# Second down pair of a decoder block: six of eleven blocks by seven products instead of five, and plain steps moved ahead of the splits of sums

## The chip, the cores and the metric

The kernel runs on one core of a Trainium2 chip. A core has five engines that work side by side and wait for each other by semaphores: TensorE (PE, matmuls), VectorE (DVE), ScalarE (ACT), GpSimd (POOL, here only an issuer of DMAs) and SyncE (SP, the issuer of most DMAs). The metric is the device time of one execution in microseconds (us), as a median of runs.

## The reference

One decoder layer on 256 tokens of width 2048, in float32. The part that the change touches is the last line: the gated activations, 256 x 5632, times `w_down`, 5632 x 2048, added to `x`.

```python
D_MODEL = 2048
SEQ = 256
D_FF = -(-(8 * D_MODEL) // (3 * 256)) * 256      # 5632
...
    x = x + merged @ w_out

    h2 = rmsnorm(x, g_ffn)
    gu = h2 @ w_gu
    x = x + (jax.nn.silu(gu[..., :D_FF]) * gu[..., D_FF:]) @ w_down
    return x
```

## The kernel before

PE multiplies in a fast format, and float32 accuracy is had by splitting each operand into a high and a low part: `split` (L109) casts the high part on ACT and subtracts it on DVE to get the low part. Each weight tile of 256 rows x 512 columns (`w_raw` or `g_raw`, 512 KB) is loaded by a DMA that SP issues, split once (`parts`, L322), and used by `product` (L177 to L179), three matmuls of 512 columns for each 128 x 128 piece of activations. The five pairs of `w_hi` and `w_lo` buffers are how far the splits can run ahead of PE.

The down projection is done in two pairs of 512 columns each (`down_pair`, L1163 on): the first call makes columns 0 to 1023, the second 1024 to 2047. The 5632 rows are eleven blocks of 512. A block's part in a pair is a 2 x 2 product of quarters (two halves of 128 tokens, two halves of 256 rows, two halves of 512 columns), and there are two ways to do it:

- plain, four steps (`rest`): a weight quarter is split and meets both halves of tokens, 12 matmuls a step, 48 in all;
- by sevens (`seven`): a scheme of seven products instead of eight. Each `form` splits one quarter or one sum of quarters and multiplies it by one piece of activations or of their sums, 6 matmuls a form, 42 in all. Its weights are b11 (form 1), u = b11 + b12 (form 5), u + b22 (form 6), b22 (form 3), b21 (form 2), b12 + b22 (form 7) and u + b22 + b21 (form 4). In the second pair the first two sums are made by DVE (L1203, L1207), the sum b12 + b22 (L1223) and the last sum of u (L1229) by DMAs that add into their target, issued by POOL; in the last block by sevens that last sum is DVE's (L1227).

Blocks 4, 6 and 8 have their sums of activations from the first pair. The second pair also takes blocks 3 and 5 by sevens: when a plain block (0, 1) is done, `sums_again` reads the raw activations of block 3 or 5 back (`a_raw`), re-makes the sums by four small differences on DVE (L231 to L236) and splits them into the done block's buffers.

`by_sevens` is a generator over the blocks by sevens. In the second pair every `yield True` (or `yield bool(again)`) in `seven` lets one plain step be written there, so that the long plain steps stand among the short forms. A scheduler at build time then sets the order on each engine from this order of writing; `tc.keep_in_program_order` holds an instruction at its place.

Of the kernel before, what the change touches and what calls it, by code (L numbers as in the profile page):

```python
# [30 lines left out]
NB = 512  # L31
# [25 lines left out]
def hybrid_block(ctx: ExitStack, tc: tile.TileContext, x, w_in, w_branch, w_out, w_gu, w_down, rel_bias,  # L57
                 onehot, extra, across, factors, out):
    nc = tc.nc
# [32 lines left out]
    def half_kb(dt=F32):  # L92

        return scratch.tile([P, NB], dt, name="sc")
# [77 lines left out]
    def product(ps, ah, al, wh, wl, start=False, stop=False, half=None):  # L172
        how = dict(skip_group_check=True)
        wh, wl = woven(wh), woven(wl)
        if half is not None:
            ps, wh, wl = ps[:, HALVES[half]], *(a[:, half * NB // 4:(half + 1) * NB // 4] for a in (wh, wl))
        nc.tensor.matmul(ps, ah, wh, start=start, stop=False, **how)  # L177
        nc.tensor.matmul(ps, ah, wl, start=False, stop=False, **how)  # L178
        nc.tensor.matmul(ps, al, wh, start=False, stop=stop, **how)  # L179
# [136 lines left out]
    def load(w, k, col0, pl=None):  # L316

        raw = pl.tile([P, 2, NB], F32, name="g_raw", bufs=6 if pl is gx else 4) if pl else wpool.tile([P, 2, NB], F32, name="w_raw", bufs=4)
        (nc.sync.dma_start if w is w_down else fetch)(raw, block(w, k, col0))
        return raw  # L320

    def parts(src):  # L322
        hi = wpool.tile([P, 2, NB], F32R, name="w_hi")
        lo = wpool.tile([P, 2, NB], F32R, name="w_lo")
        with tc.issue_after(fence.pop().ins) if fence else nullcontext():
            split_last[:] = split(hi, lo, src)
        advance(stages)
        split_count[0] += 1
        if split_count[0] % 2:
            advance(slow_stages)  # L330
        return hi, lo
# [5 lines left out]
    def snapshot(ps):  # L337
        sb = half_kb()
        nc.scalar.copy(sb, ps)  # L339
        return sb  # L340
# [709 lines left out]
    WD = (4, 6, 8)  # L1050
# [101 lines left out]
    def sums_again(c, room):  # L1152
        raw = pr.tile([P, 4, S], F32, name="a_raw", bufs=2)
        nc.gpsimd.dma_start(raw, a_mem[c])
        for _ in range(4):
            yield
        sums(*(raw[:, :, t * P:(t + 1) * P] for t in range(NT)), True)
        yield
        split(*a.t[room], raw, True)
        a.s[c] = a.t[room]  # L1160
        yield

    def down_pair(c0, mine, spare, queues, sevenths, again={}):  # L1163


        own = dict(zip(((0, 0), (1, 0), (0, 1), (1, 1)), mine()))
        begun, apart = set(), []
        xc = {}
        for t in range(NT):
            for n in range(2):  # L1170
                xc[t, n] = half_kb()
                nc.gpsimd.dma_start(xc[t, n], x1[t, :, c0 + n * NB:c0 + (n + 1) * NB])

        def into(ps, lhs, wh, wl, last=False, half=None):
            for j in range(2):
                product(ps, *lhs(j), wh[:, j], wl[:, j], id(ps) not in begun, last and j == 1, half)
                begun.add(id(ps))

        def rest(c, n, kh, last=False):
            k = 4 * c + 2 * kh  # L1180
            wh, wl = parts(load(w_down, k, c0 + n * NB))
            for t in range(NT):
                if last and again and n and t:
                    begun.discard(id(apart[0]))
                    for half, ps in enumerate((own[t, n], apart[0])):
                        into(ps, lambda j: a.plain(t, k + j), wh, wl, last, half)
                else:
                    into(own[t, n], lambda j: a.plain(t, k + j), wh, wl, last)

        def form(ps, f, c, src, last=False):  # L1190
            wh, wl = parts(src)
            into(ps, lambda j: a.form(f, c, j), wh, wl, last)

        def seven(c, f1, f5, f6, f7, last):
            def quarter(kh, n):
                return load(w_down, 4 * c + 2 * kh, c0 + n * NB, gd)

            b11 = quarter(0, 0)
            form(f1, 1, c, b11, last)
            yield bool(again)  # L1200
            b12 = quarter(0, 1)
            u = gd.tile([P, 2, NB], F32, name="u", bufs=1)
            tc.keep_in_program_order(nc.vector.tensor_add(u, b11, b12))  # L1203
            form(f5, 5, c, u, last)
            yield bool(again)
            b22 = quarter(1, 1)
            nc.vector.tensor_add(u, u, b22)  # L1207
            if not again:
                form(f6, 6, c, u, last)
                yield  # L1210
                nc.vector.tensor_add(b12, b12, b22)
                form(f7, 7, c, b12, last)
                yield
                form(own[0, 1], 3, c, b22)
                yield
                b21 = quarter(1, 0)
                form(own[0, 0], 2, c, b21)
                yield
                nc.vector.tensor_add(u, u, b21)
                form(own[1, 0], 4, c, u)  # L1220
                yield
                return
            nc.gpsimd.dma_start(b12, b22, accum_op=ALU.add)  # L1223
            form(f6, 6, c, u, last)
            b21 = quarter(1, 0)
            if last:
                tc.keep_in_program_order(nc.vector.tensor_add(u, u, b21))  # L1227
            else:
                nc.gpsimd.dma_start(u, b21, accum_op=ALU.add)  # L1229
            yield True  # L1230
            form(own[0, 1], 3, c, b22)
            yield
            form(own[0, 0], 2, c, b21)
            yield
            form(f7, 7, c, b12, last)
            yield True
            form(own[1, 0], 4, c, u)
            yield

        def combine(f1, f5, f6, f7):  # L1240

            s1 = snapshot(f1)
            nc.vector.tensor_add(xc[0, 0], xc[0, 0], s1)
            nc.vector.tensor_add(s1, f6, s1)
            s3 = half_kb()
            nc.vector.tensor_add(s3, f7, s1)
            s5 = snapshot(f5)
            yield
            nc.vector.tensor_add(xc[1, 0], xc[1, 0], s3)
            nc.vector.tensor_sub(s1, s5, s1)  # L1250
            nc.vector.tensor_add(xc[0, 1], xc[0, 1], s1)
            nc.vector.tensor_sub(s3, s5, s3)
            nc.vector.tensor_add(xc[1, 1], xc[1, 1], s3)
            yield

        def by_sevens():
            f = spare()
            apart.extend(f[:1] if again else ())
            for c in sevenths:
                yield from seven(c, *f, c == sevenths[-1])  # L1260
            yield from combine(*f)

        sevens = by_sevens()
        plain = [(c, n, kh) for c in ORDER if c not in sevenths for kh in range(2) for n in range(2)]
        if not again:
            for i, at in enumerate(plain[:-4]):
                rest(*at)
                if i >= 6:
                    next(sevens, None)
        steps = iter(plain[:-4] if again else [])  # L1270
        for now in sevens:
            at = next(steps, None) if now else None
            if at:
                rest(*at)
                if at[0] in again and at[1:] == (1, 1):
                    stages.append(sums_again(again[at[0]], at[0]))
        for at in steps:
            rest(*at)
        for n in range(2):
            for kh in range(2):  # L1280
                rest(plain[-1][0], n, kh, kh == 1)
            for t in range(NT):
                y = xc[t, n]
                if apart and t and n:
                    nc.vector.tensor_add(y, own[t, n], y)
                for half, cols in enumerate(HALVES):
                    if not (apart and t and n):
                        nc.vector.tensor_add(y[:, cols], own[t, n][:, cols], y[:, cols])
                    elif half:
                        nc.vector.tensor_add(y[:, cols], apart[0][:, cols], y[:, cols])  # L1290
                    queues[half].dma_start(
                        out[t * P:(t + 1) * P, c0 + n * NB + cols.start:c0 + n * NB + cols.stop], y[:, cols])
# [5 lines left out]
        return [acc2.tile([P, NB], F32, name=n) for n in "zv"] + [tr.tile([P, NB], F32, name="tr") for _ in range(2)]  # L1298

    down_pair(0, in_acc, elsewhere, (nc.scalar, nc.gpsimd), WD)  # L1300
    down_pair(2 * NB, elsewhere, in_acc, (nc.sync, nc.scalar), WD + (3, 5), {0: 3, 1: 5})


_INS = ["x", "w_in", "w_branch", "w_out", "w_gu", "w_down", "rel_bias"]
# [33 lines left out]
```

## Time and profile before

| | |
|---|---|
| runs | 1335.63, 1335.96, 1336.26 us, median 1335.96 |
| profiled execution | 1335.64 us, of it 1333.9 us span from first to last instruction |
| PE busy | 1327.6 us, 100% of the span |
| DVE busy | 1176.0 us, 88% |
| ACT busy | 946.2 us, 71% |
| DMA reading and writing HBM | 232 GB/s over the span |
| second down pair on PE | from 1222.67 us to the end |

An engine's busy time says how much of the span it had an instruction at work. PE is full in every slice, so where PE never waits the time follows from its number of matmuls. Whether another engine is close to making it wait has to be read from the order of time in a stage.

### The profile page before, as it was taken

What the parts mean: (1) busy time and instruction counts of PE and PEld (TensorE: products, weight loads), DVE (VectorE), ACT (ScalarE), POOL (GpSimd) and SP (SyncE); (2) the same over time, 40 slices, a digit from 0 to 9 for tenths busy, and PEclk for the clock granted to TensorE, in tenths of its full rate; (3) what the DMA queues carried; (4) which work ended last, traced back from release to release, by engine and by line L of the source; (5) the groups of instructions that cost most, each with busy time, mean ns of one, the idle gap of its engine ahead of it and who ended that gap; (6) DMA issues with size and microseconds to landing.
All of it is one profiled execution on the core that took longest, in us unless ns stands there. A gap on an engine that the chain in (4) does not pass through costs nothing.

```text
span 1333.9 us, 17798 instructions
## 1 busy us (share of the span) xinstructions
PE 1327.6 (100%) x6243; PEld 1158.4 (87%) x6243; DVE 1176.0 (88%) x1261; ACT 946.2 (71%) x1216; POOL 132.4 (10%) x197
## 2 busy tenths in 40 slices
PE   9999999999999999999999999999999999999998
PEld 6888888888888888888888888888888888888887
DVE  7978898989888897888999999998889997998887
ACT  6786867788777776546778778777877876665563
POOL 1100110001111111110210000001000001001010
PEclk9999999999999999999999999999999999999999
DMA  9987977897789878887988889889899977789893
GB/s 359 307 284 243 263 211 256 254 282 215 263 267 289 275 245 276 297 304 255 284 314 268 273 257 275 234 260 302 280 286 278 270 222 256 250 276 303 269 273 96
DMA packets 119793, 355.75 MB, mean 267 GB/s; under 512 B 32864, under 2 KB 34584, under 8 KB 119704
## 3 DMA queue, kind: packets, MB, share of 16 engines
q1 hardware_dynamic: 77016, 277.45, 57.9%
q0 software_dynamic: 20272, 70.81, 22.7%
q10 hardware_dynamic: 22416, 6.36, 3.0%
q8 instruction: 49, 0.80, 0.2%
q14 instruction: 40, 0.33, 0.1%
HBM read 294.26 MB, written 14.70 MB: 232 GB/s over the span
## 4 chain that ended last, share of the span: by engine, by line
PE 97%; DVE 1%; DMA 1%; ACT 0%; issue 0%; SPq 0%; DVEq 0%; ACTq 0%
PE qs L178 12%; PE qs L177 12%; PE qs L179 12%; PE ps L178 11%; PE ps L179 11%; PE ps L177 11%; PE z L177 4%; PE z L179 4%; PE z L178 4%; PE v L177 3%; PE v L179 3%; PE v L178 3%; PE tr L179 1%; PE tr L177 1%; PE tr L178 1%; PE tr L210 1%
## 5 line engine op out<-in xcount | busy, mean ns | idle before, releaser
L109 DVE TENSOR_TENSOR w_lo<-w_raw,w_hi 128x1024 fp32r<-128x1024 f32 x298 | 361.5, 1222 | 45.6 <-ACT w_hi L109 44.4
L109 ACT CAST w_hi<-w_raw 128x1024 fp32r<-128x1024 f32 x298 | 309.3, 1047 | 95.8 <-PE qs L179 26.0
L109 ACT CAST w_hi<-g_raw 128x1024 fp32r<-128x1024 f32 x220 | 227.0, 1050 | 105.7 <-PE qs L179 32.9
L109 DVE TENSOR_TENSOR w_lo<-g_raw,w_hi 128x1024 fp32r<-128x1024 f32 x220 | 262.7, 1223 | 19.4 <-ACT w_hi L109 16.9
L109 ACT CAST w_hi<-u 128x1024 fp32r<-128x1024 f32 x165 | 172.1, 1049 | 116.9 <-DVE u L1203 21.3
L109 DVE TENSOR_TENSOR w_lo<-u,w_hi 128x1024 fp32r<-128x1024 f32 x165 | 199.8, 1224 | 45.0 <-ACT w_hi L109 40.1
L178 PE MATMUL qs<-w_lo,h_hi 128*128 128x512 f32 x348 | 132.6, 381 | 0.0
L179 PE MATMUL qs<-w_hi,h_lo 128*128 128x512 f32 x348 | 132.1, 379 | 0.0
L178 PE MATMUL ps<-w_lo,h_hi 128*128 128x512 f32 x336 | 128.0, 381 | 0.5 <-DVE w_lo L109 0.5
L179 PE MATMUL ps<-w_hi,h_lo 128*128 128x512 f32 x336 | 127.4, 380 | 0.1
L177 PE MATMUL qs<-w_hi,h_hi 128*128 128x512 f32 x348 | 127.4, 382 | 0.0
L177 PE MATMUL ps<-w_hi,h_hi 128*128 128x512 f32 x336 | 123.1, 382 | 0.0
L406 POOL DMA_DIRECT2D u<-g_raw x47 | 40.9, 871 | 375.6 <-DVE w_lo L109 311.2
L177 PEld LDWEIGHTS qs<-w_hi,h_hi 128*128 128x128 f32 x348 | 65.7, 189 | 9.5 <-ACT sc L339 0.4
L178 PEld LDWEIGHTS qs<-w_lo,h_hi 128*128 128x128 f32 x348 | 65.8, 189 | 9.2
L179 PEld LDWEIGHTS qs<-w_hi,h_lo 128*128 128x128 f32 x348 | 65.8, 189 | 9.2
L178 PEld LDWEIGHTS ps<-w_lo,h_hi 128*128 128x128 f32 x336 | 63.5, 189 | 9.9 <-DVE w_lo L109 1.3
L179 PEld LDWEIGHTS ps<-w_hi,h_lo 128*128 128x128 f32 x336 | 63.5, 189 | 9.9 <-DVE h_lo L109 1.1
L177 PEld LDWEIGHTS ps<-w_hi,h_hi 128*128 128x128 f32 x336 | 63.3, 189 | 9.2 <-ACT h_hi L109 0.6
L355 DVE TENSOR_TENSOR u<-g_raw 128x1024 f32<-128x1024 f32 x47 | 57.4, 1223 | 10.3 <-DMA g_raw<-in_w_gu 7.6
L344 DVE TENSOR_TENSOR u<-u,g_raw 128x1024 f32<-128x1024 f32 x47 | 55.5, 1220 | 0.0
L400 POOL DMA_DIRECT2D g_raw<-g_raw x21 | 18.2, 865 | 255.5 <-DMA g_raw<-in_w_in 104.3
(442 smaller groups left out, 2982.3 us busy)
## 6 DMA issues: line engine op xcount, KB each, us to landing
w_raw<-in_w_in SPq DMA_DIRECT2D x103, 512.0 KB, 7.1
g_raw<-in_w_in SPq DMA_DIRECT2D x88, 512.0 KB, 6.1
g_raw<-in_w_gu SPq DMA_DIRECT2D x88, 512.0 KB, 6.1
w_raw<-in_w_gu SPq DMA_DIRECT2D x88, 512.0 KB, 6.5
w_raw<-in_w_down SPq DMA_DIRECT2D x56, 512.0 KB, 4.9
u<-g_raw POOLq DMA_DIRECT2D x51, 512.0 KB, 6.1
w_raw<-in_w_branch SPq DMA_DIRECT2D x32, 512.0 KB, 4.8
g_raw<-in_w_down SPq DMA_DIRECT2D x32, 512.0 KB, 5.1
```

Source lines behind the costliest of these rows:

```text
L109: cast, rest = nc.scalar.copy(hi, src), nc.vector.tensor_sub(lo, src, hi.bitcast(F32))
L177: nc.tensor.matmul(ps, ah, wh, start=start, stop=False, **how)
L178: nc.tensor.matmul(ps, ah, wl, start=False, stop=False, **how)
L179: nc.tensor.matmul(ps, al, wh, start=False, stop=stop, **how)
L210: nc.tensor.transpose(pt[:, i, :], src[:, i * P:(i + 1) * P], ident)
L344: tc.keep_in_program_order(nc.vector.tensor_add(d, d, a))
L355: nc.vector.tensor_add(d, a, b)
L400: nc.gpsimd.dma_start(d, a, accum_op=ALU.add)
L406: nc.gpsimd.dma_start(d, a, accum_op=ALU.add)
```

## The change

Block 7 goes from plain to sevens in the second pair; its activations are read back and re-made into the buffers of block 2, as blocks 3 and 5 have those of 0 and 1. In `seven` the places for plain steps change: none after form 1, one between the sum u = b11 + b12 and its split, one between the sum u + b22 and its split in the first four blocks, one after form 7, none after form 6.

```diff
@@ -1191,20 +1191,23 @@
-        def seven(c, f1, f5, f6, f7, last):
+        def seven(c, f1, f5, f6, f7, last, places):
             def quarter(kh, n):
                 return load(w_down, 4 * c + 2 * kh, c0 + n * NB, gd)
 
             b11 = quarter(0, 0)
             form(f1, 1, c, b11, last)
-            yield bool(again)
+            yield places > 3
             b12 = quarter(0, 1)
             u = gd.tile([P, 2, NB], F32, name="u", bufs=1)
             tc.keep_in_program_order(nc.vector.tensor_add(u, b11, b12))
+            if again:
+                yield True
             form(f5, 5, c, u, last)
-            yield bool(again)
+            if not again:
+                yield
             b22 = quarter(1, 1)
-            nc.vector.tensor_add(u, u, b22)
+            total = nc.vector.tensor_add(u, u, b22)
...
             nc.gpsimd.dma_start(b12, b22, accum_op=ALU.add)
+            tc.keep_in_program_order(total)
+            yield places > 2
             form(f6, 6, c, u, last)
             b21 = quarter(1, 0)
             if last:
                 tc.keep_in_program_order(nc.vector.tensor_add(u, u, b21))
             else:
                 nc.gpsimd.dma_start(u, b21, accum_op=ALU.add)
-            yield True
+            yield
...
-            for c in sevenths:
-                yield from seven(c, *f, c == sevenths[-1])
+            for i, c in enumerate(sevenths):
+                yield from seven(c, *f, c == sevenths[-1], (3 if i < 4 else 2) if again else 0)
...
-    down_pair(2 * NB, elsewhere, in_acc, (nc.sync, nc.scalar), WD + (3, 5), {0: 3, 1: 5})
+    down_pair(2 * NB, elsewhere, in_acc, (nc.sync, nc.scalar), WD + (3, 5, 7), {0: 3, 1: 5, 2: 7})
```

The build turns this into another order on DVE. A round here runs from one block's low split for form 6 to the next block's, so there are five from the first of six blocks by sevens to the last; below stands the part of a round from the low split for form 4 on; `w_lo<-u` is a low split of a sum, `w_lo<-g_raw` that of a quarter used as it is, `w_lo<-w_raw` that of a plain step, L1203 the sum b11 + b12, L1207 (L1210 after the change) the sum u + b22, and `lo_...<-a_raw` the low split of re-made sums of activations. First the fourth round of the kernel before, on DVE, in the second down pair:

```order
L109 TENSOR_TENSOR w_lo<-u,w_hi 128x1024
L109 TENSOR_TENSOR w_lo<-g_raw,w_hi 128x1024
L109 TENSOR_TENSOR w_lo<-w_raw,w_hi 128x1024
L1203 TENSOR_TENSOR u<-g_raw 128x1024
L109 TENSOR_TENSOR w_lo<-u,w_hi 128x1024
L109 TENSOR_TENSOR w_lo<-w_raw,w_hi 128x1024
L1207 TENSOR_TENSOR u<-u,g_raw 128x1024
L109 TENSOR_TENSOR w_lo<-u,w_hi 128x1024
```

Each of the two sums of u is followed at once by its own split, and a plain split stands ahead of each sum. Now the fourth round of the changed kernel on DVE:

```order
L109 TENSOR_TENSOR w_lo<-u,w_hi 128x1024
L109 TENSOR_TENSOR w_lo<-g_raw,w_hi 128x1024
L1203 TENSOR_TENSOR u<-g_raw 128x1024
L109 TENSOR_TENSOR w_lo<-w_raw,w_hi 128x1024
L109 TENSOR_TENSOR w_lo<-u,w_hi 128x1024
L1210 TENSOR_TENSOR u<-u,g_raw 128x1024
L109 TENSOR_TENSOR w_lo<-u,w_hi 128x1024
```

One plain low split is gone, and the other now stands between the first sum and that sum's split. The fifth round of the changed kernel reads the same but for a low split of re-made sums, `a_lo_6423<-a_raw`, behind the split of form 1 and a small piece of the combination (L1248) behind L1210. Next the second round of the changed kernel on DVE:

```order
L109 TENSOR_TENSOR w_lo<-u,w_hi 128x1024
L109 TENSOR_TENSOR lo_6419<-a_raw,hi_6418 128x1024
L109 TENSOR_TENSOR w_lo<-g_raw,w_hi 128x1024
L1203 TENSOR_TENSOR u<-g_raw 128x1024
L109 TENSOR_TENSOR w_lo<-w_raw,w_hi 128x1024
L109 TENSOR_TENSOR w_lo<-u,w_hi 128x1024
L109 TENSOR_TENSOR w_lo<-w_raw,w_hi 128x1024
L1210 TENSOR_TENSOR u<-u,g_raw 128x1024
L109 TENSOR_TENSOR w_lo<-u,w_hi 128x1024
```

The low split of the re-made sums of block 3 stands second, and the plain split stands ahead of the sum of L1210 rather than behind it. Last the third round of the changed kernel on DVE, from the low split for form 4:

```order
L109 TENSOR_TENSOR w_lo<-u,w_hi 128x1024
L234 TENSOR_TENSOR a_raw<-a_raw 128x2x128
L109 TENSOR_TENSOR w_lo<-g_raw,w_hi 128x1024
L1203 TENSOR_TENSOR u<-g_raw 128x1024
L235 TENSOR_TENSOR a_raw<-a_raw 128x2x128
L109 TENSOR_TENSOR w_lo<-w_raw,w_hi 128x1024
L236 TENSOR_TENSOR a_raw<-a_raw 128x2x128
L109 TENSOR_TENSOR w_lo<-u,w_hi 128x1024
L109 TENSOR_TENSOR w_lo<-w_raw,w_hi 128x1024
L1210 TENSOR_TENSOR u<-u,g_raw 128x1024
L109 TENSOR_TENSOR lo_6421<-a_raw,hi_6420 128x1024
L109 TENSOR_TENSOR w_lo<-u,w_hi 128x1024
```

The differences that re-make block 5's sums (L234 to L236) have spread into this round, the plain split is again ahead of L1210, and the low split of the re-made sums stands between L1210 and the low split for form 6.

## Rows read from the trace of the kernel before

**Rows 1.** Page: span, busy engines, granted clock by slice, chain by engine.

```profile
span 1333.9 us, 17798 instructions
...
PE 1327.6 (100%) x6243; PEld 1158.4 (87%) x6243; DVE 1176.0 (88%) x1261; ACT 946.2 (71%) x1216; POOL 132.4 (10%) x197
...
PEclk9999999999999999999999999999999999999999
...
PE 97%; DVE 1%; DMA 1%; ACT 0%; issue 0%; SPq 0%; DVEq 0%; ACTq 0%
```

**Rows 2.** PE's waits, whole program: us in total, times, longest us.

```profile
PE tr L442 <- DVE sc L457: 1.1, 1, 1.1
...
PE ps L178 <- DVE w_lo L109: 0.5, 2, 0.3
```

**Rows 3.** PE in order of time, form 6 of the first block: start, length.

```profile
1230.66 0.38 PE L178 MATMUL qs<-w_lo,a_shi 128*128 128x512 f32 x1
1230.88 0.38 PE L179 MATMUL qs<-w_hi,a_slo 128*128 128x512 f32 x1
```

**Rows 4.** Busy time by stage: us, then each engine, PEclk, DMA share, GB/s.

```profile
1237.00:1256.40 19.40, 19.40 (x92) 16.98 (x91) 17.56 (x18) 11.94 (x12) 1.72 (x2) 1.00 0.84 246
...
1275.80:1295.20 19.40, 19.40 (x92) 16.98 (x91) 15.41 (x14) 11.12 (x12) 1.70 (x2) 1.00 0.92 274
```

**Rows 5.** DVE in order of time: start, length, instruction [idle before, releaser].

```profile
1224.65 1.22 DVE L109 TENSOR_TENSOR w_lo<-u,w_hi 128x1024 fp32r<-128x1024 f32 x1
...
1244.04 0.42 DVE L231 TENSOR_TENSOR a_raw<-a_raw 128x256 f32<-128x256 f32 x1
...
1250.20 1.22 DVE L109 TENSOR_TENSOR lo<-a_raw,hi 128x1024 fp32r<-128x1024 f32 x1
...
1285.58 1.23 DVE L109 TENSOR_TENSOR w_lo<-u,w_hi 128x1024 fp32r<-128x1024 f32 x1 [1.20 <-ACT w_hi L109]
...
1294.17 1.22 DVE L109 TENSOR_TENSOR w_lo<-u,w_hi 128x1024 fp32r<-128x1024 f32 x1 [1.21 <-ACT w_hi L109]
1295.40 1.23 DVE L109 TENSOR_TENSOR w_lo<-g_raw,w_hi 128x1024 fp32r<-128x1024 f32 x1
1296.54 1.22 DVE L109 TENSOR_TENSOR w_lo<-w_raw,w_hi 128x1024 fp32r<-128x1024 f32 x1
1297.67 1.22 DVE L1203 TENSOR_TENSOR u<-g_raw 128x1024 f32<-128x1024 f32 x1
1300.09 1.23 DVE L109 TENSOR_TENSOR w_lo<-u,w_hi 128x1024 fp32r<-128x1024 f32 x1 [1.20 <-ACT w_hi L109]
...
1302.37 1.22 DVE L1207 TENSOR_TENSOR u<-u,g_raw 128x1024 f32<-128x1024 f32 x1
...
1304.76 1.23 DVE L109 TENSOR_TENSOR w_lo<-u,w_hi 128x1024 fp32r<-128x1024 f32 x1 [0.56 <-ACT w_hi L109]
...
1307.03 1.22 DVE L1227 TENSOR_TENSOR u<-u,g_raw 128x1024 f32<-128x1024 f32 x1
...
1311.57 0.69 DVE L1244 TENSOR_TENSOR sc<-qs,sc 128x512 f32<-128x512 f32 x1
```

**Rows 6.** POOL in order of time: the fourth block's add into u.

```profile
1287.10 0.85 POOL L1229 DMA_DIRECT2D u<-g_raw  x1 [6.04 <-DVE w_lo L109]
```

**Rows 7.** Line L1229, the adds into u of the second pair: landing.

```profile
L1229 POOL DMA_DIRECT2D u<-g_raw x4: 849/850/882, 1226.4 to 1287.1; - x4
...
DMA to landing us min/median/max: 5.8/5.9/7.2
```

**Rows 8.** ACT in order of time: casts for form 4, second and fourth block.

```profile
1254.25 1.04 ACT L109 CAST w_hi<-u 128x1024 fp32r<-128x1024 f32 x1 [1.41 <-DMA u<-g_raw]
...
1293.09 1.04 ACT L109 CAST w_hi<-u 128x1024 fp32r<-128x1024 f32 x1 [1.40 <-PE v L179]
```

**Rows 9.** Line L1223, the adds into b12 of the second pair: landing.

```profile
DMA to landing us min/median/max: 5.0/7.6/8.2
```

## Prediction

> **What bounds the kernel now.** I read the page first, then the waits of TensorE (PE), then its busy time by stage, then the orders of time of VectorE (DVE), ScalarE (ACT) and GpSimd (POOL) in the second down pair. The page gives a span of 1333.9 us in which PE is busy all the time, has 97% of the chain that ended last, and holds a granted clock of full speed in every slice [rows 1]. In the whole program PE waits for another engine a handful of times, 1.1 us the longest [rows 2], and the list of waits of the second down pair holds none of PE. Its starts there are 0.216 us apart [rows 3]. So time is the number of matmuls times 0.216 us, for as long as every weight split is there when PE comes to it. How near that is to failing is not in PE's rows. In three successive stretches of 19.4 us (the first and the last are shown), each as long as a block by sevens with its four plain steps, DVE is busy 15.4 to 17.6 us and the DMA engines 0.84 to 0.92 of the time [rows 4]. DVE has room by its sum; what counts is the chain of waits inside a block.
>
> That chain is the subject of the prediction, so here it is from the rows of the fourth block. DVE starts the low split for form 6 at 1285.58 [rows 5]. When that ends POOL starts the DMA that adds b21 into u, at 1287.10 [rows 6]. It lands some 5.85 us later, shortest and median of four such adds being 5.8 and 5.9 [rows 7]; ACT starts the cast of the new u for form 4 at 1293.09 (a buffer freed by PE came just after the landing here; in the second block, at 1254.25, the landing itself came last) [rows 8], and DVE its low split at 1294.17 [rows 5]. From low split 6 to low split 4 that is 8.59 us. Then DVE works through form 4, the next block's form 1, a plain step and the sum u = b11 + b12 at 1.135 us each (1295.40, 1296.54, 1297.67), waits 1.20 us since ACT can cast u only after the sum, does form 5 (1300.09), a plain step, the sum u + b22 (1302.37), and form 6 of the next block at 1304.76 [rows 5]. The round is 19.18 us. PE needs for the same round 42 matmuls of a block and 48 of four plain steps, 90 x 0.216 = 19.4 us. They are level, and PE has a small lead: in the first block the low split that starts at 1224.65 ends at 1225.88 and PE reads it at 1230.66, 4.8 us later [rows 3, 5].
>
> **The change, part by part.**
> Block 7 goes from plain to sevens. Plain it costs 4 steps x 12 matmuls, by sevens 7 forms x 6: six matmuls fewer, 6 x 0.216 = 1.3 us of PE. This is the only gain there can be, since PE has no wait in this stage to lose.
>
> Splits: 7 in place of 4, three more casts and low splits, two more sums by DVE, two more DMA adds (one stays a sum by DVE in the last block), and one more read and re-making of a block's sums. Loads stay 44. Of this, what lies in the chain is costed below.
>
> The plain steps move. There were 20 for five blocks, 4 each. Now there are 16: three for each of the first four blocks, two for each of the last two. Between low split 6 of one block and that of the next PE now gets (42 + 36) x 0.216 = 16.85 us three times and (42 + 24) x 0.216 = 14.26 us twice: 79.1 us over the five rounds.
>
> The DVE round shrinks less. A plain low split now stands between a sum and the cast that waits for it, which takes away the 1.20 us of waiting; one plain split, 1.135 us, is gone; the other changes of place fall into waits. New round: 8.59 (low split 6 to low split 4, nothing in it changed) + 4 x 1.135 (form 4, form 1, the sum, a plain step) + 0.15 (what is left of the wait for the cast of u: 2.42 from sum to low split, by 1297.67 and 1300.09, less two pitches) + 1.135 (form 5) + 2.39 (sum to low split 6, by 1302.37 and 1304.76) = 16.8 us [rows 5]. The second plain step of a round lies in the last 2.39 us when it stands behind the sum, and costs nothing there. By the order of the changed kernel:
> - round 1: sum, then plain. 16.8.
> - round 2: the plain step stands ahead of the sum, so the wait for the cast is bare again: +1.135; the low split of block 3's re-made sums stands behind form 4: +1.135, as long as the one at 1250.20 [rows 5]. 19.1.
> - round 3: plain ahead of the sum, +1.135; three of the four small differences that re-make sums stand in the chain, 0.42 us long and some 0.36 apart with the overlap that all DVE rows show (1.22 long, 1.135 apart) [rows 5]: +1.1. Their low split lies in the last wait. 19.0.
> - round 4: two plain steps only. 16.8.
> - round 5: a low split of re-made sums behind form 1: 17.9.
>
> Together 89.6 us, against 79.1 that PE takes. PE's lead of 4.8 us is used up and PE waits the rest: 89.6 - 79.1 - 4.8 = 5.7 us, in pieces under 2 us from the third round on. Behind the last low split 6 DVE has two more things to do per four forms than PE can cover (the sum u + b21 at 1307.03, and a 0.69 us piece of the combination like that at 1311.57 [rows 5]; four forms of PE give back 4 x 0.16): 0 to 1.2, I take 0.6.
>
> Sum: -1.3 + 5.7 + 0.6 = +5.0 us. The profiled execution took 1335.64, 0.32 under the median of the runs, so 1340.6 there and **1341.0** for the median.
>
> Bounds. The price that carries this is the landing of a DMA add, five times in the rounds. The shortest seen is 5.0 us (the other add, into b12, median 7.6, longest 8.2) [rows 9], the longest add into u 7.2 [rows 7]. At 5.0 each round is 0.85 shorter: 4.3 less waiting, +0.7 us in all. At 7.2 each is 1.35 longer: +11.7. I take 5.85, because shortest and median of the four adds into u, in just this place beside loads, are within 0.1 of it. The third read of activations stands in POOL's queue ahead of an add into b12; it waits for a low split that DVE does before the sum which that add needs anyway, so I cost it at nothing; without that cover it would push an add by its 0.85 us of issue.
>
> One rule speaks against the 5.85. The Trainium skill, "DMA: Bandwidth & Descriptors", section "Anatomy of one DMA — SWDGE (gpsimd) path", puts such a transfer at about 2.0 us and its bytes at 436 GB/s; for 512 KB that makes, as an estimate, 3.2 us. By it each round would be some 2.65 us shorter, 76.3 against 79.1, and PE would wait for nothing: 1334.7. The rows of adds, 5.0 at the least, do not agree with it, and the measured row decides.
>
> **The rivals.**
> *Only PE counts (faster).* The round stays under PE's, and six matmuls are simply gone: -1.3, 1334.7. For it: twelve splits and sums of 1.135 us fill 13.6 of a round's 16.85 us, and PE is busy 100%. Against: the chain is in series and busy shares don't see it. It decides if five rounds come to under 79.1 + 4.8 = 83.9, that is, adds land in about 4.7 us. [...] Chance 0.04.
> *Side work hides.* The re-made sums and the plain steps ahead of a sum fall into the waits for adds after all: 1.135 + 1.1 + 1.135 and part of the two bare plain splits, some 4 us less: +0 to +2.6, 1336 to 1338.6. For it: the adds leave DVE idle 1.2 us a round now. Against: the order puts them behind the add, not before. Adds at 5.0 us end here too. Chance 0.12.
> *Adds land late.* Six blocks now ask for eleven adds and three reads in less time than five asked for nine and two, on engines 0.92 busy; at 7.2 us a round the time is 1344 to 1348. Chance 0.10.
> *The change does not put the plain step ahead of the split.* The order shows that it does in every block; in the second and third round both plain steps stand ahead of the second sum, which is in the price above.
>
> **How the numbers follow.** My forecast, chains of 16.8 to 19.1 us with adds near 5.85, has 0.74: 1338.6 to 1344. Cut at 0.2% (2.7 us, about what a measurement of this kernel can tell from no change): slower 0.74 + 0.10 = 0.84, same 0.12 and most of the 0.04 = 0.15, faster 0.01, since the whole gain there can be is 0.1%. The range that leaves out no more than 2 in 10 reaches into hidden side work below and to the edge of late adds above: 1337.3 to 1344.2.
>
> **What the profile after would show.** Right: PE has waits on casts and low splits of u and of weights in the last 60 us, 5 to 7 us in all, none before; adds into u start 17 to 19 us apart; ACT waits for the add into u in every block, and hardly for the first sum any more. Wrong: no waits of PE and adds landing under 5 us (only PE counts), or adds above 6.5 us (late). The forecast would be off if the lead at the first block's form 6 were not near 5 us, or if the waits lowered PE's granted clock, which the one 1.1 us wait of before did not.

## The result, and the profile after

The changed kernel took 1343.32 us (median of 6 runs, 1342.50 to 1344.26) against 1335.8 for the kernel before (6 runs, 1334.62 to 1336.26): ratio 1.0058, 95% interval 1.0045 to 1.0071. It is slower, by 7.5 us.

The page of the changed kernel, with the lines that answer to [rows 1]:

```profile
span 1342.4 us, 17811 instructions
...
PE 1331.0 (99%) x6237; PEld 1158.7 (86%) x6237; DVE 1184.5 (88%) x1271; ACT 949.2 (71%) x1220; POOL 134.8 (10%) x200
...
PEclk9999999999999999999999999999999999999999
...
PE 84%; DVE 6%; DMA 4%; issue 3%; ACT 1%; POOL 0%; SPq 0%; ACTq 0%; DVEq 0%; POOLq 0%
```

PE is still busy 99% of the span and keeps its clock, but it holds only 84% of the chain that ended last, where it had 97%: VectorE's share rose from 1% to 6% and that of the DMAs from 1% to 4%. Where PE waits is in the waits of the second down pair (total us, times, longest us):

```profile
ACT w_hi L109 <- DMA u<-g_raw: 11.1, 5, 4.3
...
ACT w_hi L109 <- DVE u L1203: 9.4, 5, 2.1
ACT w_hi L109 <- DMA g_raw<-g_raw: 6.3, 4, 3.2
...
PEld tr L177 <- ACT w_hi L109: 2.7, 4, 0.8
PEld ps L177 <- ACT w_hi L109: 2.6, 3, 1.1
...
PE ps L177 <- ACT w_hi L109: 1.4, 3, 0.7
PE tr L177 <- ACT w_hi L109: 1.4, 3, 0.5
...
PE v L178 <- DVE w_lo L109: 1.0, 2, 0.8
```

Before, this list held no row of PE. Now PE and its weight loads (PEld) wait for casts and low splits, in pieces of at most 1.1 us. The first row below is where PE reads the first block's low split 6; the other two are successive starts of PE with a wait between them, for the cast of u = b11 + b12 for the fourth block's form 5:

```profile
1231.50 0.38 PE L178 MATMUL qs<-w_lo,a_shi 128*128 128x512 f32 x1
...
1276.81 0.38 PE L177 MATMUL tr<-w_hi,a_hi 128*128 128x512 f32 x1
1277.87 0.48 PE L177 MATMUL ps<-w_hi,hi 128*128 128x512 f32 x1 [0.69 <-ACT w_hi L109]
```

That cast, on ScalarE, had itself waited for the sum (L1203):

```profile
1276.78 1.04 ACT L109 CAST w_hi<-u 128x1024 fp32r<-128x1024 f32 x1 [2.08 <-DVE u L1203]
```

From 1276.81 to 1277.87 is 1.06 us instead of 0.216. All such gaps between PE's starts from 1215 us to the end add up to 8.82 us; six matmuls fewer give 1.29 back. PE's last matmul starts 8.39 us later than in the profiled execution of before (1338.48 against 1330.09): 7.53 by these two numbers, and 0.84 that was already there at 720 us, where the kernels are the same.

The chain of a round, on DVE: every low split for form 6 and for form 4, from the first block by sevens to the last (start, length, instruction, idle before it and its releaser).

```profile
1224.85 1.23 DVE L109 TENSOR_TENSOR w_lo<-u,w_hi 128x1024 fp32r<-128x1024 f32 x1
...
1235.44 1.23 DVE L109 TENSOR_TENSOR w_lo<-u,w_hi 128x1024 fp32r<-128x1024 f32 x1 [1.60 <-ACT w_hi L109]
...
1243.80 1.23 DVE L109 TENSOR_TENSOR w_lo<-u,w_hi 128x1024 fp32r<-128x1024 f32 x1
...
1253.72 1.23 DVE L109 TENSOR_TENSOR w_lo<-u,w_hi 128x1024 fp32r<-128x1024 f32 x1
...
1264.24 1.23 DVE L109 TENSOR_TENSOR w_lo<-u,w_hi 128x1024 fp32r<-128x1024 f32 x1 [1.20 <-ACT w_hi L109]
...
1272.83 1.23 DVE L109 TENSOR_TENSOR w_lo<-u,w_hi 128x1024 fp32r<-128x1024 f32 x1 [1.90 <-ACT w_hi L109]
...
1283.07 1.23 DVE L109 TENSOR_TENSOR w_lo<-u,w_hi 128x1024 fp32r<-128x1024 f32 x1
...
1292.28 1.22 DVE L109 TENSOR_TENSOR w_lo<-u,w_hi 128x1024 fp32r<-128x1024 f32 x1 [3.44 <-ACT w_hi L109]
...
1300.63 1.22 DVE L109 TENSOR_TENSOR w_lo<-u,w_hi 128x1024 fp32r<-128x1024 f32 x1 [1.19 <-ACT w_hi L109]
...
1308.04 1.23 DVE L109 TENSOR_TENSOR w_lo<-u,w_hi 128x1024 fp32r<-128x1024 f32 x1
...
1317.51 1.23 DVE L109 TENSOR_TENSOR w_lo<-u,w_hi 128x1024 fp32r<-128x1024 f32 x1 [0.57 <-ACT w_hi L109]
```

The first, third, fifth row and so on are the low splits for form 6. The five rounds between them are 18.95, 20.44, 18.83, 17.56 and 16.88 us, together 92.66. The rows between are those for form 4, which come 10.59, 9.92, 8.59, 9.21 and 7.41 us after the low split 6 ahead of them. What sits in that stretch is the add into u by DMA; its line in the changed kernel, with issue time, first and last start, and landing:

```profile
L1234 POOL DMA_DIRECT2D u<-g_raw x5: 849/854/885, 1226.6 to 1302.2; - x5
...
DMA to landing us min/median/max: 4.7/6.5/7.7
```

And the landing of the adds into b12, for ScalarE's third row of waits above:

```profile
DMA to landing us min/median/max: 6.4/8.1/9.4
```

Against [rows 7] and [rows 9] both are later by median and longest. The add into b12 makes PE wait too. In the fifth round it is this landing, and not that into u, which holds the cast for form 7, and PE's next start waits for that cast; first the cast on ScalarE, then PE's start, which comes 0.78 us later than its pitch of 0.216:

```profile
1304.25 1.04 ACT L109 CAST w_hi<-g_raw 128x1024 fp32r<-128x1024 f32 x1 [1.76 <-DMA g_raw<-g_raw]
```

```profile
1305.35 0.48 PE L177 MATMUL qs<-w_hi,hi 128*128 128x512 f32 x1 [0.62 <-ACT w_hi L109]
```

### The profile page after: what moved, and what is told of

It is laid out like the page before. It is cut to its first block, busy times and chain, and to the rows that moved or that the text cites. A ratio compares the mean times of both kernels' runs of the same rounds, so it can differ in the third digit from the quotient of the medians.

```text
span 1342.4 us, 17811 instructions
## 1 busy us (share of the span) xinstructions
PE 1331.0 (99%) x6237; PEld 1158.7 (86%) x6237; DVE 1184.5 (88%) x1271; ACT 949.2 (71%) x1220; POOL 134.8 (10%) x200
## 4 chain that ended last, share of the span: by engine, by line
PE 84%; DVE 6%; DMA 4%; issue 3%; ACT 1%; POOL 0%; SPq 0%; ACTq 0%; DVEq 0%; POOLq 0%
PE qs L178 11%; PE qs L177 11%; PE qs L179 11%; PE ps L178 10%; PE ps L179 10%; PE ps L177 10%; PE z L178 4%; PE z L177 4%; PE z L179 4%; DVE w_lo L109 3%; DMA u<-g_raw 2%; PE v L177 2%; PE v L179 2%; PE v L178 2%; ACT w_hi L109 1%
## 5 line engine op out<-in xcount | busy, mean ns | idle before, releaser
L109 DVE TENSOR_TENSOR w_lo<-w_raw,w_hi 128x1024 fp32r<-128x1024 f32 x294 | 356.3, 1220 | 45.9 <-ACT w_hi L109 44.5
L109 ACT CAST w_hi<-w_raw 128x1024 fp32r<-128x1024 f32 x294 | 305.0, 1047 | 95.8 <-PE qs L179 27.3
L109 ACT CAST w_hi<-g_raw 128x1024 fp32r<-128x1024 f32 x224 | 231.1, 1050 | 108.7 <-DVE g_raw L344 31.6
L109 DVE TENSOR_TENSOR w_lo<-g_raw,w_hi 128x1024 fp32r<-128x1024 f32 x224 | 267.6, 1221 | 21.3 <-ACT w_hi L109 18.8
L109 ACT CAST w_hi<-u 128x1024 fp32r<-128x1024 f32 x168 | 175.2, 1048 | 119.4 <-PE qs L179 20.7
L109 DVE TENSOR_TENSOR w_lo<-u,w_hi 128x1024 fp32r<-128x1024 f32 x168 | 203.3, 1222 | 44.4 <-ACT w_hi L109 38.8
```

The source lines that it names most:

```text
L109: cast, rest = nc.scalar.copy(hi, src), nc.vector.tensor_sub(lo, src, hi.bitcast(F32))
```

## The experiments

Ten kernels were run, in three groups, each timed beside the kernel before. Three theories stood: (1) the chain in series, with the landing of the add into u in it; (2) VectorE simply has too much work; (3) the DMA engines are crowded by adds. "Sum 4" is the last sum of u, u + b21 for form 4, and "sum 7" is b12 + b22. The table gives for each the first and last low split 6 (L109, `w_lo<-u`) and their distance, all gaps between PE's starts from 1215 us on beyond 0.216 us (those above 0.02 us added up), and the ratio to the kernel before with its 95% interval. The five rounds hold 79.1 us of PE's work; with five blocks it is four rounds and 77.8.

| kernel | low split 6, first to last | rounds | PE's gaps | ratio |
|---|---|---|---|---|
| changed kernel | 1224.85 to 1317.51 | 92.66 | 8.82 | 1.0058 (1.0045 to 1.0071) |
| five blocks, new places | 1226.48 to 1308.55 | 82.07 | 0.94 | 1.0001 (0.9992 to 1.0010) |
| six blocks, old places | 1221.28 to 1319.34 | 98.06 | 13.48 | 1.0093 (1.0079 to 1.0107) |
| sum 4 by DVE | 1224.27 to 1312.93 | 88.66 | 4.85 | 1.0030 (1.0019 to 1.0040) |
| both sums by DVE | 1229.91 to 1319.16 | 89.25 | 6.25 | 1.0035 (1.0021 to 1.0049) |
| sum 7 by DVE | 1223.54 to 1316.97 | 93.43 | 10.43 | 1.0064 (1.0051 to 1.0077) |
| a quarter of the add | 1224.81 to 1315.90 | 91.09 | 7.85 | 1.0034 (1.0021 to 1.0046) |
| no side work | 1224.02 to 1311.78 | 87.76 | 7.37 | 1.0032 (1.0019 to 1.0044) |
| no side work, sum 4 by DVE | 1225.37 to 1308.64 | 83.27 | 0.00 | 0.9986 (0.9976 to 0.9996) |
| side work on GpSimd, sum 4 by DVE | 1224.20 to 1313.65 | 89.45 | 5.69 | 1.0032 (1.0019 to 1.0044) |
| side work on GpSimd | 1224.79 to 1319.70 | 94.91 | 11.26 | 1.0075 (1.0061 to 1.0089) |

### The two halves of the change

Five blocks again, only the places moved (with four plain steps a block, the fourth place is the one behind form 1, as before):

```diff
-    ... c == sevenths[-1], (3 if i < 4 else 2) if again else 0)
+    ... c == sevenths[-1], 4 if again else 0)
-    down_pair(2 * NB, ..., WD + (3, 5, 7), {0: 3, 1: 5, 2: 7})
+    down_pair(2 * NB, ..., WD + (3, 5), {0: 3, 1: 5})
```

> The changed kernel with five blocks by sevens in the second down pair as before (block 7 plain again), and four places for plain steps in every block, at the changed places: only the moving of the plain steps is left. Theory 1: TensorE gets 90 matmuls a round, 19.4 us, and the chain takes 16.8 to 19.1 us and one plain split of 1.135 us, so it stays level or ahead; TensorE waits 0 to 2 us, time 1335.6 to 1338. A rival, that the new places by themselves cost (plain splits ahead of the sum in two rounds, late adds), would leave most of the 7.5 us here: 1340 or more.

Measured 1336.26 us, no difference from before within 0.1%. The four rounds came to 82.07 us, and PE's 77.8 and a lead of 5.9 cover them. The moving alone costs nothing that this shows; the sixth block does.

Six blocks, the plain steps at their old places. With three or two steps a block the place behind form 1 stays empty: they stand behind forms 5, 6 and 7, in the last two blocks behind 6 and 7:

```diff
-            if again:
-                yield True
             form(f5, 5, c, u, last)
-            if not again:
-                yield
+            yield places > 2
...
-            tc.keep_in_program_order(total)
-            yield places > 2
             form(f6, 6, c, u, last)
...
-            yield
+            yield True
             form(own[0, 1], 3, c, b22)
```

> The changed kernel with its six blocks, but the plain steps at the places they had before (behind forms 1, 5, 6 and 7; three in the first four blocks, two in the last two). Theory 1: the wait of 1.20 us of VectorE behind each first sum comes back in a round whose length already is above TensorE's work, so up to 1.2 us for each of five rounds less what the moved plain splits give back: 2 to 5 us longer than the changed kernel, 1345 to 1348. A rival, that the places do nothing and only the number of blocks counts: as the changed kernel, 1343.3 within 1.3.

Measured 1348.41 us, 5 us more than the changed kernel, just past the far end of theory 1's range and against the rival: as built, the new places pay for part of the sixth block. But only in part by the way I expected. The rounds are 5.4 us longer than those of the changed kernel; 2.8 of that stands between low split 6 and low split 4 (48.51 us in five stretches against 45.72), where theory 1 had no change, and 4.8 falls in the third round alone. What the waits of 1.20 us cost by themselves this run does not show. In the third round one wait of PE is 4.69 us long, and ScalarE's order of time shows what it goes back to: the cast of re-made sums, which waits for the differences. VectorE's low split of those sums waits for that cast, the sum b11 + b12 stands behind that split, and PE waits for the cast of that sum:

```profile
1275.04 1.04 ACT L109 CAST hi<-a_raw 128x1024 fp32r<-128x1024 f32 x1 [3.06 <-DVE a_raw L236]
```

Next the busy times of this kernel in three stretches behind it (us, PE, PEld, DVE, ACT, POOL, PEclk, DMA share, GB/s):

```profile
1276.00:1278.00 2.00, 0.00 (x0) 0.00 (x0) 1.89 (x2) 0.08 (x1) 0.00 (x0) 0.82 0.32 131
...
1280.00:1282.00 2.00, 1.84 (x4) 1.17 (x4) 2.00 (x3) 0.57 (x1) 0.00 (x0) 0.50 0.89 270
...
1284.00:1286.00 2.00, 2.00 (x10) 1.73 (x10) 1.66 (x2) 2.00 (x3) 0.14 (x1) 0.97 0.75 277
```

PE does nothing in the first of them, and then its granted clock is 0.50, the lower of its two levels (1.2 GHz), until about 1284 us.

### The last sum of u by VectorE

```diff
-            if last:
-                tc.keep_in_program_order(nc.vector.tensor_add(u, u, b21))
-            else:
-                nc.gpsimd.dma_start(u, b21, accum_op=ALU.add)
+            tc.keep_in_program_order(nc.vector.tensor_add(u, u, b21))
```

> The changed kernel, but the last sum of u (u + b21, for form 4) is made by VectorE in all six blocks, as it is in the last one; no DMA adds into u any more. Theory 1 (the chain in series: low split 6, GpSimd, the DMA add of 4.7 to 7.7 us, the cast, low split 4): each of five rounds loses 8.59 us from low split 6 to low split 4 and gets a sum of 1.135 us and the 2.4 us from a sum to its low split, 3.5 us, so some 5 us less, less what VectorE then needs for the forms that it did in that wait; rounds of 15 to 17 us, waits of TensorE in the second down pair 0 to 4 us instead of 8.8, time 1335 to 1339. Theory 2 (VectorE has too much work): five more sums of 1.135 us, 5.7 us on the busiest engine beside TensorE, so the time rises to some 1346 to 1349. Theory 3 (the DMA engines are crowded by adds): five transfers fewer, the other add lands faster than its median of 8.1 us and the time falls, as in theory 1; the two are told apart by the rounds of the kernel with the sum for form 7 by VectorE.

Measured 1340.09 us: faster than the changed kernel, as theory 1 has it, by 2.8 parts in a thousand, and theory 2's 1346 did not come. But the fall stopped 1 us short of my range. DVE's first and last low split 6 in order of time:

```profile
1224.27 1.23 DVE L109 TENSOR_TENSOR w_lo<-u,w_hi 128x1024 fp32r<-128x1024 f32 x1
...
1312.93 1.23 DVE L109 TENSOR_TENSOR w_lo<-u,w_hi 128x1024 fp32r<-128x1024 f32 x1 [1.16 <-ACT w_hi L109]
```

DVE's waits in this kernel between 1250 and 1315 us (total, times, longest):

```profile
DVE w_lo L109 <- ACT w_hi L109: 3.6, 3, 1.2
```

In those 65 us DVE waits 3.6 us. The landing of the add into u is out of the chain and DVE's own work has become the bound: its rounds of 88.66 us are 4.0 shorter, and PE's gaps 4.85 instead of 8.82.

With the sum for form 7 on DVE too (`nc.vector.tensor_add(b12, b12, b22)` in place of the DMA):

> The changed kernel with both sums that DMAs add (u + b21 and b12 + b22) made by VectorE in all six blocks; no DMA adds in the second down pair. Theory 1: no landing is left in the chain, but eleven more sums of 1.135 us stand on VectorE, 2.27 us a round; the round comes to some 14 x 1.135 us and a bare wait, 16.5 to 18 us, against PE's 16.85 and 14.26; time 1338 to 1342, between the kernel with only u by VectorE and the changed one. Theory 2 (VectorE's amount of work alone): 12.5 us more work, 1350 or more. Theory 3 (crowded DMA engines): the fastest of all, 1335 or less, since eleven transfers of 512 KB are gone.

Measured 1340.83 us, inside theory 1's range. No adds by DMA at all did not make it fast, so theory 3 falls as the whole cause; VectorE has eleven sums more here, so it is not shown that adds beside each other cost nothing. The third kernel moves only the sum for form 7:

> The changed kernel with the sum b12 + b22 (for form 7) made by VectorE in all six blocks, the last sum of u by DMA as it is. Theory 1: the sum stands right behind u + b22, in the bare wait for the cast or ahead of low split 6, and takes 0 to 1.135 us of a round; the add into u, now without the other add beside it, may land some 0.5 us sooner; 1341 to 1346. Theory 3 (DMA engines crowded by adds): six transfers of 512 KB fewer, landings of the add into u near 5 us and ScalarE's waits for the other add gone: 1337 to 1340.

Measured 1345.18 us, as theory 1 said. The adds into u landed a little sooner (5.3/5.7/7.2 us) and the rounds still grew by 0.8 us. That is a balance: the five stretches from low split 6 to low split 4 lost 1.9 us (45.72 to 43.81), and the rest of the rounds, where VectorE now makes this sum, gained 2.7. So the other add does hold up the add into u a little, and taking it away by more work for VectorE costs more than that.

### A smaller add, and the side work

```diff
-                nc.gpsimd.dma_start(u, b21, accum_op=ALU.add)
+                nc.gpsimd.dma_start(u[:, :, :P], b21[:, :, :P], accum_op=ALU.add)
```

> The changed kernel, but the DMA adds only the first 128 of 512 columns of b21 into u, 128 KB in place of 512 KB (three quarters of that sum are left out); its place, its wait and its reader stay. Only the landing gets shorter, and the DMA engines carry 1.9 MB less. Theory 1: each round gets shorter by what the landing loses, until the other work of VectorE fills it; with landings some 2 us shorter the rounds lose up to 10 us and TensorE's waits fall from 8.8 to 0 to 4 us: 1335 to 1339. Theory 2 (VectorE's amount of work): as the changed kernel, 1343.

Measured 1341.40 us, above theory 1's 1335 to 1339. The dose was smaller than I had thought; the line in this kernel:

```profile
L1234 POOL DMA_DIRECT2D u<-g_raw x5: 1198/1205/1229, 1226.6 to 1299.5; - x5
...
DMA to landing us min/median/max: 4.5/5.5/6.2
```

A quarter of the bytes lands only 1.0 us sooner by the median, and GpSimd is busy 0.35 us longer with issuing it. The five landings lost 4.5 us together, but from low split 6 to low split 4 the five stretches lost only 1.57 (45.72 to 44.15), the rounds the same 1.57, and PE's gaps 0.97. In the first, third and fourth stretch, where low split 4 waits for the landing, the landings lost 2.5 us and the stretches 2.3. In the second and fifth VectorE was not idle ahead of low split 4 even in the changed kernel (its rows at 1253.72 and 1308.04 show no wait), and there 2.0 us less of landing came with stretches 0.75 us longer: VectorE first waited 1.15 and 1.34 us for the cast of b12 + b22 and then had its side work to do. So theory 1 holds where this landing comes last, and the other add and VectorE's work set the rest.

Without the side work, that is without `sums_again`'s read, differences and split:

```diff
-        raw = pr.tile([P, 4, S], F32, name="a_raw", bufs=2)
-        nc.gpsimd.dma_start(raw, a_mem[c])
...
-        sums(*(raw[:, :, t * P:(t + 1) * P] for t in range(NT)), True)
...
-        split(*a.t[room], raw, True)
-        a.s[c] = a.t[room]
+        a.s[c] = a.s[4]
```

> The changed kernel without the side work: blocks 3, 5 and 7 use block 4's sums of activations in place of their own, so nothing is read back, no small differences are made and no sums are split (that part of the computation is left out; forms, loads, splits of weights and matmuls stay). It takes 3 reads of 512 KB, 12 differences of about 0.36 us and 3 low splits of 1.135 us away, 7.7 us of VectorE's work. Theory 1 (chain in series): what stood in series goes, by my sum 1.135 + 1.1 + 1.135 in the rounds and a little behind them, 3 to 5 us: 1338.5 to 1340.5. Theory 2 (VectorE's amount of work): all 7.7 us, 1335 to 1336. A rival, that side work lies in waits and is hidden: 1342 or more.

Measured 1340.91 us, 0.4 above my range. The rounds shrank by 4.9 us as expected, but up to PE's reading of the last low split 6 its gaps were 3.19 us and behind that 4.18 instead of the 0.75 of the changed kernel. ScalarE's order of time there shows why:

```profile
1316.01 1.04 ACT L109 CAST w_hi<-g_raw 128x1024 fp32r<-128x1024 f32 x1 [1.89 <-DMA g_raw<-g_raw]
```

PE's next two starts behind that cast:

```profile
1317.11 0.48 PE L177 MATMUL qs<-w_hi,a_shi 128*128 128x512 f32 x1 [1.41 <-ACT w_hi L109]
1318.06 0.82 PE L177 MATMUL tr<-w_hi,a_hi 128*128 128x512 f32 x2 [0.46 <-ACT w_hi L109]
```

And PE in three stretches around them (us, busy, granted clock, DMA share, GB/s):

```profile
1314.00:1316.00 2.00, 1.70 (x8) 1.00 0.11 23
...
1320.00:1322.00 2.00, 2.00 (x6) 0.52 0.65 197
1322.00:1324.00 2.00, 2.00 (x11) 1.00 0.16 66
```

The add into b12 had become the late one: ScalarE waited 1.89 us for it, PE's start at 1317.11 came 1.57 us and the next 0.73 us later than its pitch, and from 1318.67 to 1321.66 its starts were 0.43 us apart, at a granted clock near 0.5. Seven such starts cost 7 x 0.21 = 1.5 us.

Both edits together:

> The two edits together: no side work (same part left out) and the last sum of u by VectorE in all six blocks, no add into u. In the kernel with that sum by VectorE alone, VectorE had hardly a wait left from 1250 us on, five rounds of 88.7 us against TensorE's 79.1 and a lead of 4.8. If the limit there is VectorE's work, 7.7 us less leaves rounds of about 81 us, TensorE waits for nothing and the six matmuls are gained: 1334.4 to 1335.5. If it is the other add (into b12, landing 8 us) or the loads, waits of 3 us or more stay: 1338 or more.

Measured 1334.69 us, 0.9 us under the kernel before as timed beside it (1335.59), and the only one that gains. The first and last low split 6:

```profile
1225.37 1.23 DVE L109 TENSOR_TENSOR w_lo<-u,w_hi 128x1024 fp32r<-128x1024 f32 x1
...
1308.64 1.23 DVE L109 TENSOR_TENSOR w_lo<-u,w_hi 128x1024 fp32r<-128x1024 f32 x1 [1.19 <-ACT w_hi L109]
```

83.27 us of rounds, PE's 79.1 and its lead of 5.4: no gap at all. From PE's 5501st matmul, ahead of the stage, to its last is 157.71 us against 159.00 in the kernel before, which is six matmuls of 0.216. So the two edits together, the landing out of the chain and the side work away, take all the waiting, and what is left is the six matmuls. The side work is more than VectorE's: with it went three casts of ScalarE and three reads by DMA, so the share of VectorE alone is argued and not shown.

### Side work on GpSimd

The same two ideas with the whole computation kept: the differences and low splits of the re-made sums go to GpSimd.

```diff
-        sums(*(raw[...] for t in range(NT)), True)
+        sums(*(raw[...] for t in range(NT)), True, nc.gpsimd)
...
-        split(*a.t[room], raw, True)
+        split(*a.t[room], raw, True, nc.gpsimd)
```

> The whole computation with six blocks, VectorE freed in the two ways that the earlier runs tried apart: the last sum of u is VectorE's in all blocks (no landing in the chain), and the small differences and low splits of the re-made sums of blocks 3, 5 and 7 are made by GpSimd, which issues only transfers otherwise. If the limits are the landing of the add into u and then VectorE's amount of work, TensorE waits for next to nothing and the six matmuls are gained, as in the run without side work: 1334.3 to 1336. A rival: GpSimd is slow at such work (no row shows its time for it) or lengthens VectorE's instructions while it works; then sums come late or VectorE's 1.23 us grow, waits of 2 us or more and 1338 or longer.

Measured 1340.22 us, no better than with sum 4 on DVE alone; the rival holds. Two of GpSimd's low splits in its order of time:

```profile
1248.70 3.44 POOL L109 TENSOR_TENSOR lo<-a_raw,hi 128x1024 fp32r<-128x1024 f32 x1 [4.44 <-ACT hi L109]
...
1268.03 2.60 POOL L109 TENSOR_TENSOR lo<-a_raw,hi 128x1024 fp32r<-128x1024 f32 x1 [10.23 <-ACT hi L109]
```

DVE's low splits at the same moments:

```profile
1249.81 3.41 DVE L109 TENSOR_TENSOR w_lo<-w_raw,w_hi 128x1024 fp32r<-128x1024 f32 x1
...
1268.30 3.41 DVE L109 TENSOR_TENSOR w_lo<-u,w_hi 128x1024 fp32r<-128x1024 f32 x1
```

And PE's longest wait in the second down pair (total, times, longest), beside the third of these splits, near 1300 us:

```profile
PE z L178 <- DVE w_lo L109: 2.6, 1, 2.6
```

DVE's low split of 1.22 us takes 3.41 while GpSimd is at its own of 3.44 and 2.60: each time DVE's ends 1.08 us after GpSimd's. The two did not work side by side here, so the work taken from DVE came back as stretched time. The Trainium skill, "Trainium Architecture — The Big Picture", section "What this means for kernel authors", says that these two engines contend for a port pair that one of them holds alone; the rows agree.

> The changed kernel with only the side work moved to GpSimd (differences and low splits of the re-made sums), the adds into u by DMA as they are. Theory 1 (the landing is in the chain): only the side work in series goes, as in the run without side work, waits of TensorE of 4 to 7 us, 1338 to 1341; GpSimd's own work ahead of a DMA add in its queue may delay one. If side work were the whole cost, 1335.

Measured 1346.05 us, above theory 1's range and no faster than the changed kernel (the intervals of the two ratios overlap); its rounds, 94.91 us, are 2.3 longer. Beside GpSimd's differences and splits VectorE's instructions took 1.6 to 3.1 us here too, and ScalarE's cast of re-made sums, with other casts behind it, waited for GpSimd's differences:

```profile
1251.13 1.05 ACT L109 CAST hi<-a_raw 128x1024 fp32r<-128x1024 f32 x1 [2.28 <-POOL a_raw L236]
```

No version with the whole computation beat the kernel before.

## Why the prediction was right, point by point

**Sign and size.** 1341.0 was forecast, 1343.3 measured, inside the range. "This is the only gain there can be" (six matmuls, 1.3 us) is shown by the run without side work and with sum 4 on DVE: where PE waits for nothing, the stage is 1.29 us shorter and the ratio is 0.9986.

**The round's model.** Rounds minus PE's work minus the lead gives PE's wait: 92.66 - 79.1 - 5.42 = 8.14, and PE's gaps up to its reading of the last low split 6 are 8.07 us. With each kernel's own lead the same subtraction comes within 0.1 us of the gaps in all nine kernels with six blocks in which PE waits. It is an account and not yet a cause: what makes the rounds long is told by the experiments. The lead was 4.8 in the working; here the first low split 6 ends at 1226.08 and PE reads it at 1231.50, 5.4 later, because PE was 0.84 us late from before the stage. Behind that reading the gaps are 0.75, where I had 0.6.

**The step that was mis-sized** is "8.59 (low split 6 to low split 4, nothing in it changed)", taken for all five rounds. They measured 10.59, 9.92, 8.59, 9.21 and 7.41, 2.8 us more together. The rest of the rounds, low split 4 to the next low split 6, measured 8.36, 10.52, 10.24, 8.35 and 9.47 against 8.2, 10.5, 10.4, 8.2 and 9.3 forecast: the order told them, bare waits and side work included, to 0.2 us. The landing was spread over 4.7 to 7.7 us where I took 5.85: in order 7.7, 7.2, 5.9, 6.5 and 4.7, and each stretch is its landing and 2.7 us more, 2.9 in the first. That the sum is off by no more is in part luck: the first, second and fourth stretch were 4.0 us longer together, the fifth 1.2 shorter. And the sum had no term for the add into b12, which made PE wait in the fifth round. The largest part, 2.0 us in the first round, was in the trace of before and I passed over it. Its first block, in the order of time of DVE; the low split 6 ahead of it is at 1224.65 [rows 5]:

```profile
1235.61 1.23 DVE L109 TENSOR_TENSOR w_lo<-u,w_hi 128x1024 fp32r<-128x1024 f32 x1 [1.36 <-ACT w_hi L109]
```

The line of the adds into u of before, in the first block alone, has this landing:

```profile
DMA to landing us min/median/max: 7.2/7.2/7.2
```

That is 10.96 us from low split 6 to low split 4, and the 7.2 that I had put down as the slowest add [rows 7] belongs to the first place; the other three land in 5.8 to 5.9. A median over four adds hid this. With 10.96 for the first stretch the sum would have been 1343.4. But 0.8 us of the 10.96 is not the landing: ScalarE's cast came that much behind it, since it waited for a buffer that PE freed, which the changed kernel's first cast did not.

```profile
1234.53 1.05 ACT L109 CAST w_hi<-u 128x1024 fp32r<-128x1024 f32 x1 [1.54 <-PE v L179]
```

Why the first add is slow was not tried. What stands beside it is known: GpSimd issues two stores of 128 KB from 1224.4 us on, up to 2 us ahead of it, in both kernels. In the kernel with the old places it issues them behind the add (1222.81, then 1223.69 on), and the add still lands in 6.9 us, so their place ahead of it in GpSimd's queue does not make it slow. Whether their transfers hold it up stays open.

**What the profile would show.** Waits of PE on casts and low splits: right, though 8.8 us and not 5 to 7, and from the second round on and not the third, since the first add is the slow one. Adds into u 17 to 19 us apart: 17.6 to 20.4. ScalarE waits for the add in every block: 11.1 us in five times. That ScalarE would hardly wait for the first sum was wrong in its own rows (9.4 us, five times), yet DVE's low split 5 follows its plain split with next to no idle, which is what the step needed. PE's granted clock did not fall.

**The rivals.** "Only PE counts" did not happen; it does when the landing in the chain and the side work are both taken away. "Side work hides" is wrong: without it the rounds are 4.9 us shorter and the time falls, by 2.4 us of medians or 0.26% of the ratios. "Adds land late" was half right: the median of 6.5 lies between my 5.85 and its 7.2, and the time 0.7 below its stretch. The places matter: with the old ones the six blocks cost 5 us more, though only in part by the waits that I had counted.

## What to carry to other kernels

An engine that is busy all the time can still lose when another engine's serial chain per round becomes longer than its work per round: subtract work and lead from the chain, and the waits come out to a tenth of a us here. Read such a chain for each round apart, not by a median; here the first round, next to the end of the stage before, was the slow one. And when a landing is taken out of the chain, ask what bounds the round next: here VectorE's own work took most of the gain back.

## What the runs showed of the hardware

The adds into u by DMA of 128 KB landed in 4.5 to 6.2 us, those of 512 KB in 4.7 to 7.7: a quarter of the size took 1.0 us off the median. VectorE and GpSimd hold each other up: 1.22 us became 3.41 beside a GpSimd instruction on tiles of the same size. A wait of PE can cost more than itself: behind the one of 4.69 us the granted clock was 0.50 for some 6 us, behind those of 1.57 and 0.73 us near 0.5 for some 3; a gap of 2.88 us in the kernel with side work on GpSimd and sum 4 on DVE was followed by none of this, the clock stayed at 1.00. And the profiled executions of kernels that are alike up to the second down pair were not level there: PE's 5501st matmul started between 1169.8 and 1172.5 us in eleven of the twelve and at 1176.2 in the one with both sums on DVE, so a profiled span alone tells less than the ratio of the runs.
